# A hybrid decoder layer on one core: seven block products two tiles earlier in the first FFN, with their results kept in PSUM

## Chip, cores and metric

One Trainium2 chip, one of its cores. The metric is the device time of one launch in microseconds, as the median of several runs. The engines are named as in the profile: PE is TensorE (matmul), PEld its weight loads, DVE is VectorE, ACT is ScalarE, POOL is GpSimd, SP is SyncE, which issues the DMA transfers.

## The reference

One layer of a decoder trunk is computed for 1024 prompt rows and for 8 single sample rows with a cache. Width is 1024, the FFNs are 2816 wide.

```python
def swiglu(x, w_gate, w_up, w_down):
    return (jax.nn.silu(x @ w_gate) * (x @ w_up)) @ w_down

def decoder_layer(x, ...):
    h = x + 0.5 * rmsnorm(swiglu(rmsnorm(x, lp['n_ffn1_pre']), lp['ffn1_gate'], lp['ffn1_up'],
                                 lp['ffn1_down']), lp['n_ffn1_post'])
    proj = rmsnorm(h, lp['n_mix_pre']) @ lp['w_in']
    ...  # differential attention (512 wide) and RWKV-7 time mixing (512 wide)
    mix = jnp.concatenate([ya, yb], axis=-1) @ lp['w_out']
    h = h + rmsnorm(mix, lp['n_mix_post'])
    h = h + 0.5 * rmsnorm(swiglu(rmsnorm(h, lp['n_ffn2_pre']), lp['ffn2_gate'], lp['ffn2_up'],
                                 lp['ffn2_down']), lp['n_ffn2_post'])
```

Everything is float32. In the kernel a matrix is held as a high part (rounded to the fp32r type) and a low part (what is left), and a product is the sum of three fp32r matmuls: high by high, high by low, low by high.

## The kernel before

**Stages.** The rows are cut into two halves of 520 (with the 8 sample rows) and 512. The trunk runs four phases: 0 and 1 are the first FFN for the first and the second half, 2 and 3 the second FFN. Between and beside them run the projection, the attention, the time mixing and the output product, as streams of their own. `s_trunk` (L1034) runs the phases. A phase takes the 22 tiles of 128 FFN columns in turn: `gate` and `up` (L1061, L1081) make the two products of a tile for two chunks of rows (256 and 264 columns of a matmul, 8 blocks of the input dimension by 3 = 24 matmuls each), VectorE and ScalarE make silu(gate) × up of them, and split the result in a high and a low part. `down` (L1166) multiplies the activations of a group of tiles by their rows of the third weight matrix and adds the result to a sum in SBUF. The groups of tiles are in `GROUPS` (L102); while one group's gate and up run, the down products of the group before follow.

**Seven block products.** In phases 0 and 3, from tile `FAST[ph]` on (L35: 8 in phase 0, 4 in phase 3), two tiles at a time go through `seven` (L1098). It writes the product of a pair (weights 1024 × 256, inputs 1024 × 520) as blocks of two by two and makes it from seven products of blocks in place of eight, twice: for the gates and for the ups. Each of the seven takes 12 matmuls (4 input blocks by 3) of 260 columns. For this the weights' blocks are added by `sums` (L940) and the inputs' blocks by `s_combine` (L994). The latter makes four sums t1 to t4 of the input's blocks, in four steps, split in high and low parts: in the trace the tiles comb_acc and comb_sq are the sums, comb_dreg and comb_T hold their high and low parts (t1 and t2 in comb_dreg, t3 and t4 in the two tiles comb_T). `seven` waits for all of that.

After each of its products VectorE adds the bank to one of four slots `v` in SBUF (L1145 to L1152). When a block of the result is complete, `gates` (L1115) multiplies it by the row norms `rb` (phase 0), takes the tanh on ScalarE and multiplies; `ups` (L1123) multiplies the gates by it, ScalarE casts the high part into the ring of activations (trunk_xl in the trace) and VectorE or GpSimd subtracts it to get the low part. Six banks of PSUM rotate for the products (m0 to m3, aux0, aux1).

**The order.** Nothing is issued in the order of the source. Each operation goes through one helper (line L325 in every row of the profile) into a queue of its stream, and `Kern.run` (L484) plans all engines by a model of costs and due times: on each engine the operation that can start first goes first, and among those within a few hundredths of a microsecond the one with the earliest due time. `either` (L432) chooses VectorE or GpSimd for an elementwise operation by the same model. The due times come from a pass before; `PASSES` (L96) counts the planning passes (L2665), and the cheapest of all but the first is built. So a change in one place can move operations anywhere in the program.

Of the kernel before, what the change touches and what calls it, by code (L numbers as in the profile page):

```python
# [13 lines left out]
F32 = mybir.dt.float32  # L14
# [4 lines left out]
ALU = mybir.AluOpType  # L19
# [12 lines left out]
SAMPLE = slice(HS, HS + TD)  # L32
CHUNKS = [[(0, 256), (256, 264)], [(0, 256), (256, 256)], [(0, 256), (256, 256)], [(0, 264), (264, 256)]]
WIDE = (1, 2)
FAST = {0: 8, 3: 4}  # L35
HALF = 260
FOUR = 1
PIECE = 2048
# [54 lines left out]
MW = 1  # L93
MARG = 0
SLACK = 0.02
PASSES = 8  # L96
BIAS = {}
SHIFT = {}
MIX = 1
# [118 lines left out]
class Kern:  # L218
# [637 lines left out]
    def plan(ph):  # L856

        groups = [[0, 1, 2], [3, 4], [5, 6]] + [list(range(g, g + 3)) for g in range(7, NF, 3)]
        if ph in FAST:
            groups = GROUPS[ph, FAST[ph]] + [[g, g + 1] for g in range(FAST[ph], NF, 2)]  # L860
        down = lambda gi: [("down", gi, m0) for m0 in range(0, KT, Kern.down_tiles(groups[gi]))]
        seq = []
        for gi, grp in enumerate(groups):
            for q, f in enumerate(grp):
                if f < FAST.get(ph, NF):
                    seq += [("gate", f, None), ("up", f, None)]
# [10 lines left out]
    def s_weights(self):  # L877
# [3 lines left out]
        for ph in range(4):  # L881
# [4 lines left out]
            for n, (kind, f, m0) in enumerate(seq):  # L886
# [7 lines left out]
                if kind[-1] == "s":  # L894
                    yield from self.sums(ph, kind, f, m0, tag, last)
                    continue
                fast = kind == "down" and groups[f][-1] + 1 >= FAST.get(ph, NF + 1)
                if fast and not FOUR:
# [24 lines left out]
                kept = None  # L923
                if ph // 2 in LOWS and (kind == "down" or f < FAST[3 * (ph // 2)]):
                    kept = self.Ld[ph // 2][grp[0]:grp[-1] + 1, :, m0 * P:m0 * P + nm].rearrange("q p m -> p q m") if kind == "down" else \
# [108 lines left out]
    def s_trunk(self):  # L1034

        nc = self.nc
        V, A, G = nc.vector, nc.scalar, nc.gpsimd
        for ph in range(4):
            groups, _ = self.plan(ph)
            if ph in FAST:  # L1040
                self.spawn(self.s_combine(ph), "comb", 3)
# [13 lines left out]
            def weights(*key):  # L1055
                if key not in got:
                    yield ("wait", ("loaded", ph) + key)
                    got[key] = self.W.pop((ph,) + key)
                return got[key]
# [38 lines left out]
            def seven(f):  # L1098

                yield ("wait", ("combined", ph))  # L1100
                if ph == 0:
                    for c in range(2):
                        yield ("wait", ("rb", c))
                gt[:] = [self.T(self.pool, [P, 2 * W], j) for j in "gt"]
                b11, b21, b22, t1, t2, t3, t4 = self.blocks
                for i in range(2):
                    acts[f + i] = act[(f + i) % 4]

                def beside(fn, *a):
                    was = self.cur  # L1110
                    self.cur = self.asides["trunk"]
                    fn(*a)
                    self.cur = was

                def gates(i, j, src):  # L1115
                    g, t = gt[i][:, HALF * j:HALF * j + HALF], self.tmp("sq", 2, HALF)
                    if ph == 0:
                        V.tensor_tensor(g, src, self.rb[:, HALF * j:HALF * j + HALF], ALU.mult)
                        src = g
                    A.activation(t, src, AF.Tanh, scale=0.5)  # L1120
                    V.scalar_tensor_tensor(g, t, 1.0, src, ALU.add, ALU.mult)

                def ups(i, j, src):  # L1123
                    g = gt[i][:, HALF * j:HALF * j + HALF]
                    o = 1040 * ((f + i) % 4) + HALF * j
                    ah, al = (ring[:, o + w:o + w + HALF] for w in (0, 520))
                    V.tensor_tensor(g, g, src, ALU.mult)
                    A.copy(ah, g)
                    self.either("tensor_tensor", al, g, ah.bitcast(F32), ALU.subtract)

                for kind, use in (("gates", gates), ("ups", ups)):
                    v = [self.vs[(self.nv + i) % len(self.vs)] for i in range(4)]
                    self.nv += 4
                    late = []
                    for n, (j, i, x) in enumerate(((0, 0, b11), (0, 1, b21), (1, 0, t2), (1, 1, t3), (2, 0, t4), (2, 1, t1), (3, 0, b22))):
                        wh, wl = yield from weights(kind, f, j)
                        ps = self.ps(HALF)
                        for k in range(4):
                            self.mm3(ps, wh[:, i, k, :], wl[:, i, k, :], x[0][k], x[1][k], k == 0, k == 3)
                            if k == 1:  # L1140
                                yield "pe"
                        if i or j == 3:
                            self.signal(("used", ph, kind, f, j))
                        was, late = late, []
                        if n == 0:  # L1145
                            A.copy(v[0], ps)
                        elif n == 5:
                            V.tensor_tensor(v[2], v[2], ps, ALU.add)
                            V.tensor_tensor(v[0], v[0], ps, ALU.add)
                        else:  # L1150
                            o, a = ((1, 0), (0, 0), (2, 0), (3, 2), (0, 0), (0, 0))[n - 1]
                            V.tensor_tensor(v[o], v[a], ps, ALU.add)  # L1152
                        q = {1: (0, 0, 1), 4: (1, 0, 3), 5: (1, 1, 2), 6: (0, 1, 0)}.get(n)
                        if q:
                            late.append((use, q[0], q[1], v[q[2]]))
                        for fn, *a in was:
                            beside(fn, *a)
                        yield "pe"
                    for fn, *a in late:
                        beside(fn, *a)  # L1160
                if f + 2 == NF:
                    self.signal(("ups", ph))
                    if ph == 0:
                        self.spawn(self.s_resid(ph), "resid", 0)
# [1510 lines left out]
```

## Time and profile before

| what | value |
|---|---|
| median of 3 runs | 2241.66 us (2240.61 to 2243.62) |
| the profiled execution's own time | 2243.7 us |
| its span | 2241.9 us, 42167 instructions |
| granted TensorE clock, mean | 0.994 |
| DMA | 338.84 MB, 151 GB/s over the span |

The span is the stretch from the first to the last instruction of the profiled execution. All engines run side by side; an engine's busy time is the sum of its instructions' durations, and the time of the kernel is set by the engine that never waits, or by the chain of waits from one engine to the next. Where a row says "[2.59 <-DVE mix_T L325]", the engine had been idle for 2.59 us and went on when VectorE had written the tile mix_T.

### The profile page before, as it was taken

To read this page: it belongs to the slowest core of one execution; us is meant where nothing else is said; L and a number is where in the kernel's file an instruction comes from. 1 tells how busy PE (TensorE), PEld (TensorE's weight loads), DVE (VectorE), ACT (ScalarE), POOL (GpSimd) and SP (SyncE) were. 2 spreads that over 40 slices of the span, in tenths; PEclk is the share of its full clock that TensorE was granted. 3 is DMA by queue.
4 is the path that set the end of the run, shared out by engine and by line. 5 is a ranking of instruction groups with operands and counts; after the bars stand their busy time and mean duration, and the time that the engine had idled before them with its cause. 6 is when DMAs were issued, how large, how long until landed. Compare 5 with 4: busy or idle time off the path is not lost. (4 is left out here: it accounts for less than half of the span.)

```text
span 2241.9 us, 42167 instructions
## 1 busy us (share of the span) xinstructions
PE 2187.3 (98%) x15551; PEld 1960.6 (87%) x15551; DVE 1559.9 (70%) x3608; ACT 1085.1 (48%) x2233; POOL 1007.8 (45%) x834
## 2 busy tenths in 40 slices
PE   8999999999999989999999999999999999999998
PEld 8999998899887778898887777778888989999998
DVE  7868887656667787647775667776765366777776
ACT  6434444644553347344454445435655455444444
POOL 4545555533333673456453332335443355444443
PEclk9999999999999999999999999999999999999999
DMA  7322233445343674755564534476337838342343
GB/s 262 111 95 87 94 113 124 132 149 140 100 116 103 190 213 132 218 156 164 164 205 156 145 115 129 136 221 199 114 103 220 275 115 290 118 151 99 138 147 108
DMA packets 216088, 338.84 MB, mean 151 GB/s; under 512 B 50731, under 2 KB 130379, under 8 KB 215883
## 3 DMA queue, kind: packets, MB, share of 16 engines
q1 hardware_dynamic: 215594, 335.63, 47.9%
q8 instruction: 123, 2.02, 0.4%
q14 instruction: 83, 0.67, 0.1%
q10 hardware_dynamic: 288, 0.52, 0.1%
HBM read 281.06 MB, written 55.03 MB: 150 GB/s over the span
## 5 line engine op out<-in xcount | busy, mean ns | idle before, releaser
L325 POOL TENSOR_TENSOR wts_w<-wts_raw,wts_w 128x1024 fp32r<-128x1024 f32 (+2 forms) x160 | 301.2, 1886 | 356.8 <-ACT wts_w L325 301.1
L325 PE MATMUL trunk_m<-trunk_xl,wts_w 128*128 128x256 f32 (+2 forms) x2574 | 421.7, 316 | 0.4 <-DVE trunk_xl L325 0.4
L325 PE MATMUL trunk_m<-pre_X,wts_w 128*128 128x512 f32 (+3 forms) x2040 | 390.0, 344 | 9.6 <-ACT wts_w L325 6.0
L325 PEld LDWEIGHTS trunk_m<-trunk_xl,wts_w 128*128 128x128 f32 x2574 | 359.3, 188 | 29.4 <-issue 1.6
L325 PE MATMUL trunk_m<-pre_T,wts_w 128*128 128x512 f32 (+3 forms) x1800 | 364.6, 353 | 6.7 <-DVE trunk_xl L325 6.6
L325 PEld LDWEIGHTS trunk_m<-pre_X,wts_w 128*128 128x128 f32 x2040 | 312.8, 190 | 51.7 <-ACT wts_w L325 6.0
L325 ACT CAST wts_w<-wts_raw 128x512 fp32r<-128x512 f32 (+3 forms) x299 | 242.3, 826 | 211.1 <-PE trunk_m L325 123.0
L325 PEld LDWEIGHTS trunk_m<-pre_T,wts_w 128*128 128x128 f32 x1800 | 285.1, 191 | 47.3 <-issue 4.9
L325 PE MATMUL proj_m<-tail_xl,lin_w 128*128 128x256 f32 (+2 forms) x1920 | 320.9, 322 | 0.5 <-DVE init_E L325 0.5
L325 PEld LDWEIGHTS proj_m<-tail_xl,lin_w 128*128 128x128 f32 x1920 | 270.7, 188 | 35.0 <-issue 9.6
L325 DVE TENSOR_TENSOR trunk_xl<-trunk_xl,trunk_m 128x256 f32<-128x256 f32 (+2 forms) x362 | 172.5, 490 | 53.1 <-PE trunk_m L325 52.2
L325 POOL TENSOR_TENSOR lin_w<-lin_raw,lin_w 128x1024 fp32r<-128x1024 f32 x41 | 99.7, 2432 | 221.4 <-ACT lin_w L325 211.4
L325 POOL TENSOR_TENSOR trunk_xl<-trunk_t,trunk_xl 128x260 fp32r<-128x260 f32 (+3 forms) x87 | 93.7, 1078 | 132.9 <-ACT trunk_xl L325 128.9
L325 DVE TENSOR_TENSOR wts_w<-wts_raw,wts_w 128x1024 fp32r<-128x1024 f32 (+3 forms) x109 | 114.1, 1052 | 13.9 <-ACT wts_w L325 13.5
L325 POOL TENSOR_TENSOR wts_w<-wts_lraw,wts_w 128x512 fp32r<-128x512 f32 x57 | 78.5, 1380 | 60.1 <-ACT wts_w L325 57.4
L325 ACT CAST lin_w<-lin_raw 128x1024 fp32r<-128x1024 f32 x52 | 54.5, 1047 | 74.6 <-PE proj_m L325 54.0
L325 PE MATMUL trunk_m<-comb_T,wts_w 128*128 128x260 f32 x660 | 84.7, 283 | 0.0
L325 PEld LDWEIGHTS trunk_m<-comb_T,wts_w 128*128 128x128 f32 x660 | 81.7, 188 | 0.0
L325 ACT CAST wts_w<-wts_lraw 128x512 fp32r<-128x512 f32 x100 | 58.7, 619 | 38.5 <-POOL wts_lraw L325 12.5
L325 PE MATMUL trunk_aux<-trunk_xl,wts_w 128*128 128x256 f32 (+1 forms) x546 | 75.1, 282 | 0.0
L325 ACT CAST trunk_xl<-trunk_t 128x512 fp32r<-128x512 f32 (+3 forms) x94 | 45.4, 484 | 50.4 <-DVE trunk_t L325 49.7
L325 PEld LDWEIGHTS trunk_aux<-trunk_xl,wts_w 128*128 128x128 f32 x546 | 69.5, 189 | 0.0
(614 smaller groups left out, 4088.0 us busy)
## 6 DMA issues: line engine op xcount, KB each, us to landing
wts_raw<-in_ffn_gate_dram SPq DMA_DIRECT2D x87, 512.0 KB
wts_raw<-in_ffn_up_dram SPq DMA_DIRECT2D x56, 512.0 KB
lin_raw<-in_w_in_dram SPq DMA_DIRECT2D x52, 512.0 KB
wts_raw<-in_ffn_down_dram SPq DMA_DIRECT2D x52, 384.0 KB
wts_raw<-in_ffn_down_dram SPq DMA_DIRECT2D x31, 512.0 KB
wts_w<-Ld SPq DMA_DIRECT2D x22, 512.0 KB
wts_lraw<-in_ffn_down_dram SPq DMA_DIRECT2D x18, 512.0 KB
mix_T<-out_dram SPq DMA_DIRECT2D x36, 256.0 KB
```

What stands on the lines that cost most here:

```text
L325: o = Op(eng, lambda: fn(*a, **k), st)
```

## The change

Three parts. In phase 0 the seven block products begin with tile 6 in place of tile 8: the groups of tiles go from [0,1,2], [3,4], [5], [6,7] and seven pairs to [0,1,2], [3], [4,5] and eight pairs. The products' results stay in the bank of PSUM: two slots in SBUF in place of four for each kind, the sums that complete a block are written into the bank, and all that follows (norm, tanh, multiplication, cast, subtraction) reads it there; the subtraction is always VectorE's. And the planner makes nine passes in place of eight.

```diff
-FAST = {0: 8, 3: 4}
+FAST = {0: 6, 3: 4}
...
-PASSES = 8
+PASSES = 9
...
                     if ph == 0:
-                        V.tensor_tensor(g, src, self.rb[:, HALF * j:HALF * j + HALF], ALU.mult)
-                        src = g
+                        V.tensor_tensor(src, src, self.rb[:, HALF * j:HALF * j + HALF], ALU.mult)
                     A.activation(t, src, AF.Tanh, scale=0.5)
                     V.scalar_tensor_tensor(g, t, 1.0, src, ALU.add, ALU.mult)
...
-                    V.tensor_tensor(g, g, src, ALU.mult)
-                    A.copy(ah, g)
-                    self.either("tensor_tensor", al, g, ah.bitcast(F32), ALU.subtract)
+                    V.tensor_tensor(src, g, src, ALU.mult)
+                    A.copy(ah, src)
+                    V.tensor_tensor(al, src, ah.bitcast(F32), ALU.subtract)
 
                 for kind, use in (("gates", gates), ("ups", ups)):
-                    v = [self.vs[(self.nv + i) % len(self.vs)] for i in range(4)]
-                    self.nv += 4
+                    v = [self.vs[(self.nv + i) % len(self.vs)] for i in range(2)]
+                    self.nv += 2
...
                         elif n == 5:
-                            V.tensor_tensor(v[2], v[2], ps, ALU.add)
                             V.tensor_tensor(v[0], v[0], ps, ALU.add)
+                            V.tensor_tensor(ps, v[1], ps, ALU.add)
                         else:
-                            o, a = ((1, 0), (0, 0), (2, 0), (3, 2), (0, 0), (0, 0))[n - 1]
-                            V.tensor_tensor(v[o], v[a], ps, ALU.add)
-                        q = {1: (0, 0, 1), 4: (1, 0, 3), 5: (1, 1, 2), 6: (0, 1, 0)}.get(n)
+                            o, a = ((ps, 0), (v[0], 0), (v[1], 0), (ps, 1), None, (ps, 0))[n - 1]
+                            V.tensor_tensor(o, v[a], ps, ALU.add)
+                        q = {1: (0, 0), 4: (1, 0), 5: (1, 1), 6: (0, 1)}.get(n)
                         if q:
-                            late.append((use, q[0], q[1], v[q[2]]))
+                            late.append((use, *q, ps))
```

The program has 14147 matmul rows on TensorE in place of 14171 (192 of 256 and 264 columns fewer, 168 of 260 more), 3669 rows on VectorE (3600 before), 2110 on ScalarE (2100), 803 on GpSimd (836) and 1219 on SyncE as before. On GpSimd 62 subtractions into trunk_xl are gone, and some 30 low parts of weights have come in.

The first place is TensorE's queue at the first products of the first pair that read a combined input (comb_dreg and comb_T; in brackets the engines whose counters a row waits for). Before:

```order
L325 MATMUL trunk_aux_237_1870<-comb_dreg_530,wts_w_217_1693 128x260 [waits Activation_49]
L325 MATMUL trunk_aux_237_1870<-comb_dreg_530,wts_w_217_1693 128x260 x11
L325 MATMUL trunk_m_239_1887<-comb_T_92_531,wts_w_217_1693 128x260 [waits DVE_49,Activation_49]
L325 MATMUL trunk_m_239_1887<-comb_T_92_531,wts_w_217_1693 128x260
L325 MATMUL trunk_m_239_1887<-comb_T_92_531,wts_w_217_1693 128x260 [waits Pool_49]
L325 MATMUL trunk_m_239_1887<-comb_T_92_531,wts_w_217_1693 128x260 x9
```

And of the change:

```order
L325 MATMUL trunk_aux_197_1453<-comb_dreg_530,wts_w_177_1265 128x260 [waits Activation_49]
L325 MATMUL trunk_aux_197_1453<-comb_dreg_530,wts_w_177_1265 128x260 x5
L325 MATMUL trunk_aux_197_1453<-comb_dreg_530,wts_w_177_1265 128x260 [waits Activation_49]
L325 MATMUL trunk_aux_197_1453<-comb_dreg_530,wts_w_177_1265 128x260 [waits DVE_49]
L325 MATMUL trunk_aux_197_1453<-comb_dreg_530,wts_w_177_1265 128x260
L325 MATMUL trunk_aux_197_1453<-comb_dreg_530,wts_w_177_1265 128x260 [waits Activation_49]
L325 MATMUL trunk_aux_197_1453<-comb_dreg_530,wts_w_177_1265 128x260 [waits Pool_49]
L325 MATMUL trunk_aux_197_1453<-comb_dreg_530,wts_w_177_1265 128x260
```

The third product (comb_dreg is t2) waited only at its start; now it waits for VectorE, ScalarE and GpSimd in its midst too, the last time for GpSimd at its eleventh matmul.

The second place is GpSimd's queue at the end of `s_combine` (trunk_xl is a tile's activation, wts_w a weight split, init and pre the inputs). Before:

```order
L325 TENSOR_TENSOR trunk_xl_18_121<-trunk_t_1206,trunk_xl_18_121 128x264 [waits Activation_49]
L325 TENSOR_TENSOR comb_T_93_532<-comb_sq_544,comb_T_93_532 128x260 [waits Activation_49]
L325 TENSOR_TENSOR comb_acc_545<-comb_acc_545,pre_X_47_150 128x260 [waits DVE_49,Pool_49]
L325 TENSOR_TENSOR comb_sq_547<-pre_X_46_149 128x260 [waits Pool_49]
L325 TENSOR_TENSOR comb_sq_548<-pre_X_46_149,comb_acc_546 128x260 [waits DVE_49]
L325 TENSOR_TENSOR comb_dreg_530<-comb_acc_546,comb_dreg_530 128x260 [waits Activation_49]
L325 TENSOR_TENSOR wts_w_189_1461<-wts_raw_1384,wts_w_189_1461 128x1024 [waits DMAHW4_49,Activation_49]
```

And of the change:

```order
L325 TENSOR_TENSOR trunk_xl_18_121<-trunk_t_1304,trunk_xl_18_121 128x256 [waits Activation_49]
L325 TENSOR_TENSOR comb_T_93_532<-comb_sq_544,comb_T_93_532 128x260 [waits Activation_49]
L325 TENSOR_TENSOR comb_acc_545<-comb_acc_545,pre_X_47_150 128x260 [waits DVE_49,Pool_49]
L325 TENSOR_TENSOR comb_sq_547<-pre_X_46_149 128x260
L325 TENSOR_TENSOR wts_w_196_1442<-wts_lraw_1394,wts_w_196_1442 128x512 [waits DMAHW2_49,PE_49,Activation_49]
L325 TENSOR_TENSOR comb_sq_548<-pre_X_46_149,comb_acc_546 128x260 [waits DVE_49,Pool_49]
L325 TENSOR_TENSOR comb_dreg_530<-comb_acc_546,comb_dreg_530 128x260 [waits Activation_49]
```

A weight split, which waits for TensorE and for ScalarE's cast, has moved ahead of the last two steps of the combine.

The third place is VectorE's queue at the seam between the ups of a pair and the down products (trunk_aux1, m0, m1, m2 added to trunk_xl0 are down products; trunk_xl1 is the ring of activations; the number after a name's bank tells its use). Before:

```order
L325 TENSOR_TENSOR init_rb_10_113<-init_rb_10_113,trunk_aux0_320_2484 128x260
L325 TENSOR_TENSOR trunk_xl0_126_796<-trunk_xl0_126_796,trunk_aux1_324_2506 128x256
L325 TENSOR_TENSOR trunk_xl0_126_796<-trunk_xl0_126_796,trunk_m0_325_2514 128x264
L325 TENSOR_TENSOR wts_w3_319_2473<-wts_raw_315_2435,wts_w3_319_2473 128x512
L325 TENSOR_TENSOR trunk_xl0_126_796<-trunk_xl0_126_796,trunk_m1_326_2524 128x256
L325 TENSOR_TENSOR wts_cb_322_2494<-wts_raw_316_2436 128x512
L325 TENSOR_TENSOR trunk_xl0_126_796<-trunk_xl0_126_796,trunk_m2_327_2535 128x264
```

And of the change:

```order
L325 TENSOR_TENSOR trunk_aux0_224_1682<-init_rb_10_113,trunk_aux0_224_1682 128x260
L325 TENSOR_TENSOR trunk_m3_222_1660<-trunk_t_193_1414,trunk_m3_222_1660 128x260
L325 TENSOR_TENSOR trunk_xl0_126_786<-trunk_xl0_126_786,trunk_aux1_228_1704 128x256
L325 TENSOR_TENSOR trunk_xl1_18_121<-trunk_m3_222_1660,trunk_xl1_18_121 128x260
L325 TENSOR_TENSOR trunk_aux0_224_1682<-trunk_g_192_1413,trunk_aux0_224_1682 128x260
L325 TENSOR_TENSOR trunk_xl0_126_786<-trunk_xl0_126_786,trunk_m0_229_1715 128x264
L325 TENSOR_TENSOR trunk_xl0_126_786<-trunk_xl0_126_786,trunk_m1_230_1727 128x256
L325 TENSOR_TENSOR trunk_xl1_18_121<-trunk_aux0_224_1682,trunk_xl1_18_121 128x260
```

The last product of the ups, in the bank aux0, was added into SBUF in one step and the bank was free; now the sum, the multiplication and the subtraction all happen in the bank, and the sixth down product is the next to use it.

Elsewhere the streams are interleaved anew without a clear direction: in TensorE's queue, ahead of two of the attention's products (attn_m) that read mix_T, there stand 1 matmul of the trunk (2 before) and 2 (4 before).

## The prediction

> **What bounds the kernel now.** First the page's table of engines, then the busy time by stretch. In the second view each row is a stretch of the span; the columns are its length, then each engine's busy time with its instructions, the granted TensorE clock, the DMA share and GB/s.
>
> ```profile
> PE 2187.3 (98%) x15551; PEld 1960.6 (87%) x15551; DVE 1559.9 (70%) x3608; ACT 1085.1 (48%) x2233; POOL 1007.8 (45%) x834
> core 0: us, PE busy (x) PEld busy (x) DVE busy (x) ACT busy (x) POOL busy (x), PEclk, DMA share, GB/s
> 142.50:361.00 218.50, 218.50 (x1824) 218.50 (x1823) 184.38 (x394) 93.78 (x191) 121.55 (x100) 1.00 0.32 106
> 430.00:1164.00 734.00, 718.90 (x4964) 620.67 (x4963) 500.99 (x1235) 348.01 (x713) 334.84 (x261) 1.00 0.53 158
> 1164.00:1820.00 656.00, 642.38 (x4030) 529.58 (x4029) 420.60 (x1010) 326.82 (x695) 252.58 (x168) 1.00 0.54 162
> 1877.00:2220.00 343.00, 343.00 (x2851) 342.95 (x2849) 251.31 (x533) 154.73 (x319) 158.38 (x148) 1.00 0.41 144
> ```
>
> TensorE sets the time. In the two stretches of block products (the first and the last row) it has no idle time at all, so there only fewer or shorter matmuls shorten anything. Between them it idles 734.0 − 718.9 = 15.1 us and 656.0 − 642.4 = 13.6 us, 28.7 us in all; a gain from a better order can only come from there or from the edges.
>
> **Term 1, fewer matmuls.** Then the timeline of TensorE, where seven products replace tiles (start, duration, operation, count):
>
> ```profile
> 77.10 23.14 PE L325 MATMUL trunk_m<-pre_X,wts_w 128*128 128x256 f32 x192
> 100.07 11.64 PE L325 MATMUL trunk_m<-trunk_xl,wts_w 128*128 128x256 f32 x96
> 129.57 13.09 PE L325 MATMUL trunk_m<-pre_X,wts_w 128*128 128x256 f32 x108
> 142.50 1.60 PE L325 MATMUL trunk_aux<-pre_X,wts_w 128*128 128x260 f32 x12
> ...
> 172.71 1.60 PE L325 MATMUL trunk_m<-pre_X,wts_w 128*128 128x260 f32 x12
> ...
> 192.89 0.87 PE L325 MATMUL trunk_aux<-trunk_xl,wts_w 128*128 128x256 f32 x6
> 193.60 3.03 PE L325 MATMUL trunk_m<-trunk_xl,wts_w 128*128 128x264 f32 x24
> ```
>
> Two tiles done one by one are 2 × 2 × 2 × 24 = 192 matmuls: tiles 4 and 5 take 100.07 − 77.10 = 22.97 us, 0.1196 each. A pair by seven products is 2 × 7 × 12 = 168 matmuls: 192.89 − 172.71 = 20.18 us. The change swaps tiles 6 and 7 for one more pair; their down products stay in number. **−2.8 us**, and nothing else of the edit removes TensorE work. Their weight loads, four for a pair, come up to 35 us earlier too; the pairs at 142.5 to 361 ran beside a DMA share of 0.32 without a wait, so I cost them at zero, and one late load at the 6.0 us of term 4's second row.
>
> **Term 2, the combined inputs come late.** The first seven-pair starts 35 us earlier. In before its first product begins after 96 of the 108 matmuls at 129.57, at 141.1 (the second is the row at 142.50); now after tiles 4 and 5 and the down products of tile 3 (96 + 48 + 96 matmuls), at 77.10 + 240 × 0.1196 = 105.8. The block sums of the inputs were ready at 117.0:
>
> ```profile
> 116.23 0.77 DVE L325 TENSOR_TENSOR comb_T<-comb_sq,comb_T 128x260 fp32r<-128x260 f32 x2
> ...
> 94.67 0.75 POOL L325 TENSOR_TENSOR comb_acc<-comb_acc,pre_X 128x260 f32<-128x260 f32 x1 [1.01 <-DVE comb_acc L325]
> 94.88 0.83 DVE L325 TENSOR_TENSOR comb_sq<-pre_X 128x260 f32<-128x260 f32 x1
> 97.71 0.42 DVE L325 TENSOR_TENSOR comb_sq<-comb_sq,pre_X 128x260 f32<-128x260 f32 x1
> 98.05 0.42 DVE L325 TENSOR_TENSOR comb_sq<-pre_X,comb_acc 128x260 f32<-128x260 f32 x1
> ...
> 110.42 0.74 POOL L325 TENSOR_TENSOR comb_sq<-pre_X,comb_acc 128x260 f32<-128x260 f32 x1 [3.18 <-DVE comb_acc L325]
> 111.13 0.74 POOL L325 TENSOR_TENSOR comb_dreg<-comb_acc,comb_dreg 128x260 fp32r<-128x260 f32 x1
> ```
>
> So 24 us of slack are gone and the chain must be pulled forward by the planner. The third product is the first that reads a combined tile. It starts at 105.8 + 2 × 1.44 = 108.7 (12 × 20.18 ÷ 168 = 1.44 per product), and its eleventh matmul, which waits for GpSimd's last low part, is due 10 × 0.119 = 1.2 us later, at 109.9. In the new order GpSimd has a weight split ahead of that low part. That split waits for a ScalarE cast, which waits until TensorE has left the weight buffer at the end of the second product. What such a chain takes, from rows further on:
>
> ```profile
> 204.40 1.60 PE L325 MATMUL trunk_m<-pre_X,wts_w 128*128 128x260 f32 x12
> 204.66 0.62 ACT L325 CAST wts_w<-wts_raw 128x512 fp32r<-128x512 f32 x1 [0.95 <-PE trunk_m L325]
> 205.35 1.29 POOL L325 TENSOR_TENSOR wts_w<-wts_raw,wts_w 128x512 fp32r<-128x512 f32 x1 [2.86 <-ACT wts_w L325]
> 1820.91 2.37 POOL L325 TENSOR_TENSOR wts_w<-wts_raw,wts_w 128x1024 fp32r<-128x1024 f32 x1 [1.94 <-ACT wts_w L325]
> 1823.34 3.50 PE L325 MATMUL trunk_m<-pre_X,wts_w 128*128 128x512 f32 x14 [1.45 <-POOL wts_w L325]
> ```
>
> From the end of the products to the cast 204.66 − 204.40 = 0.26, cast to GpSimd 0.69, the split 1.29, then the two steps of the combine at 0.71 (111.13 − 110.42) and 0.74, then to TensorE 1823.34 − (1820.91 + 2.37) = 0.06: 3.75 us. From 108.7 that is 112.4 against 109.9: **+2.5 us**, the third product waiting.
>
> Bounds. Below: nothing, if the ScalarE cast of the weights were not behind the second product after all (as in before, where the combine ended 24 us ahead). Above: VectorE and GpSimd slow each other when both read two tiles of SBUF: the subtraction at 94.88 took 0.83 us beside GpSimd's at 94.67, and 0.42 alone (97.71). If they went strictly in turn after the last elementwise step of tile 5 at 106.2, VectorE's eight rows left there (7 × 0.34, the step from 97.71 to 98.05, and 0.6) and GpSimd's seven (6 × 0.72 and 1.29) would sum to 8.6 us: 114.8, a stall of 4.9. I take 2.5, since it is the chain that the order itself imposes.
>
> Nothing else is queued between these on TensorE: the products behind are its own, so a stall there is time lost in full. What does a stall do to the clock?
>
> ```profile
> 824.31 0.50 PE L325 MATMUL attn_m<-mix_X 128*128 128x512 f32 x1 [2.59 <-DVE mix_T L325]
> 824.00:828.00 4.00, 3.69 (x16) 3.04 (x17) 3.67 (x7) 3.48 (x10) 1.51 (x1) 1.00 0.70 231
> 1870.10 7.59 PE L325 MATMUL trunk_m<-pre_T,wts_w 128*128 128x264 f32 x48 [2.77 <-DVE trunk_xl L325]
> 1870.00:1874.00 4.00, 3.90 (x20) 3.93 (x21) 3.13 (x8) 2.64 (x3) 3.57 (x5) 0.60 1.01 385
> 380.31 11.66 PE L325 MATMUL trunk_m<-pre_T,wts_w 128*128 128x512 f32 x38 [3.85 <-DVE trunk_xl L325]
> 378.00:382.00 4.00, 1.69 (x4) 1.43 (x5) 3.96 (x8) 0.96 (x4) 1.60 (x2) 0.65 0.00 0
> 382.00:386.00 4.00, 4.00 (x11) 3.04 (x11) 3.96 (x9) 0.22 (x1) 3.82 (x6) 0.50 0.01 4
> ```
>
> After a gap of 2.59 us the granted clock stayed 1.00; after 2.77 it was 0.60 for 4 us, 1.6 us lost; after 3.85 it was 0.65 and 0.50, 1.4 + 2.0 = 3.4 us lost. A stall of 2.5 lies just under the smallest that cost anything, so I add nothing. The Trainium skill ("TensorE: Matmul & The Clock Gate", What's actually happening) puts the window at about 3.4 us, free-running, and advises no gaps longer than that; by it alone a 2.5 us stall is free. The row at 1870.10 differs: 2.77 us did cost. Going by that row the forecast would be 1.6 us more.
>
> **Term 3, results that stay in PSUM.** The elementwise steps read and write a bank in place of SBUF:
>
> ```profile
> L325 DVE TENSOR_TENSOR init_E<-init_E,trunk_m 128x260 f32<-128x260 f32 x24 | 10.1, 423 | 8.8 <-PE trunk_m L325 8.7
> L325 DVE TENSOR_TENSOR wts_dec<-wts_cb,wts_raw 128x512 f32<-128x512 f32 x16 | 11.1, 692 | 0.0
> 194.88 0.68 DVE L325 TENSOR_TENSOR wts_w<-wts_raw,wts_w 128x512 fp32r<-128x512 f32 x1
> L325 POOL TENSOR_TENSOR trunk_xl<-trunk_g,trunk_xl 128x260 fp32r<-128x260 f32 x30 | 25.2, 839 | 38.3 <-ACT trunk_xl L325 38.3
> L325 POOL TENSOR_TENSOR trunk_xl<-trunk_t,trunk_xl 128x260 fp32r<-128x260 f32 x32 | 24.7, 772 | 32.1 <-ACT trunk_xl L325 32.1
> ```
>
> Into PSUM an operation costs what it costs into SBUF (692 ns to a bank, 0.68 us at 194.88 to SBUF; 423 ns with a PSUM input, 0.42 without): zero per instruction. What moves is the last subtraction of each result: 62 of them (30 + 32) leave GpSimd for VectorE, some 4 per pair × 0.42 = 1.7 us in a pair of 20.18 + 11.6 = 31.8 us. VectorE is busy 184.4 of 218.5 us in this stage, 4.96 us free per pair, so it is hidden beneath TensorE; without that cover it would be 1.7 us × 17 pairs.
>
> What it can cost is a bank. Six banks rotate, and one is now held until its split is done. At the seam to the down products the bank of the seventh product is due again at the sixth down product, 5 × (193.60 − 192.89) = 3.6 us later. VectorE's first row after a product, and then its seven others until the split is done:
>
> ```profile
> 193.80 0.42 DVE L325 TENSOR_TENSOR trunk_xl<-trunk_xl,trunk_aux 128x256 f32<-128x256 f32 x1 [0.28 <-PE trunk_aux L325]
> ```
>
> 193.80 − 193.60 = 0.2 to start, 7 × 0.34, then 0.42: 3.0 us, slack 0.6. It just fits: zero. One weight split of 0.68 between them, as at 194.88, would overrun by some 0.1, with ScalarE's cast in between 0.2, at each of the 17 pairs of both FFNs: +3.4. Below zero it can't go, since TensorE does not wait there now.
>
> **Term 4, the plan made anew.** All streams are interleaved afresh (one pass more), with the same work outside the first FFN. What that moves in the middle is bounded by the waits of TensorE (total, times, longest):
>
> ```profile
> PE attn_m L325 <- DVE mix_T L325: 6.3, 4, 2.6
> PE trunk_m L325 <- ACT wts_w L325: 6.0, 1, 6.0
> ```
>
> Between −6.3 (the attention's waits all filled) and +6.0 (one long wait more). The new order puts fewer matmuls of the trunk ahead of two of these waits, and nothing in it says that others grow or shrink; I take 0, as the middle keeps its work.
>
> **Sum.** −2.8 + 2.5 + 0 + 0 = −0.3 us. The profiled execution took 2243.7 us (span 2241.9 and 1.8 around it), so 2243.4 by it; the median of the runs, 2241.66, is 2.0 lower, so **2241.4**.
>
> **Rivals.** A difference under 0.2%, 4.5 us here (2237.2 to 2246.1), is about what a measurement of this kernel can tell from no change.
> - A, the sum above, 2241.4: 0.43, same.
> - E, the combine is in time, only term 1 counts: 2238.9. For it: the planner knows when the inputs are due. Against it: the weight split ahead in GpSimd's queue. 0.10, same.
> - C, the bank seam overruns in each pair: −0.3 + 3.4, 2244.8. For it: slack of 0.6 only. Against it: 34 us of free VectorE time in the stage. 0.09, same.
> - B, the other side: GpSimd and VectorE go in turn at the end of the combine, the third product stalls 4.9 us and the clock falls as at 380.31, 3.4 us more. −2.8 + 4.9 + 3.4 = +5.5, 2247.2. Slower by 4.5 needs stall and clock of 7.3, so it decides from a stall of 3.9 us. For it: 0.83 beside GpSimd against 0.42. Against it: ScalarE's and GpSimd's waits leave gaps in which VectorE runs alone. 0.20, slower.
> - D, the new plan fills the attention's waits: −0.3 − 6.3, 2235.1. For it: 28.7 us idle in the middle. Against it: fewer FFN matmuls ahead there. 0.18, faster.
>
> **Range and chances.** Low is E's 2238.9 with D's 6.3 less, about 2233; high is B with most of C, about 2250; 1 to 2 in 10 are left outside. Faster 0.22 (D, and a part of E with a little of the middle), same 0.52, slower 0.26 (B, and A or C with a longer middle).
>
> **What would show it.** Right: 24 matmuls fewer, the first 260-column product near 106 us, one TensorE gap of about 2.5 us in the third product, put down to GpSimd's combined tile, the clock at 1.00 after it, and no gaps in the following pairs. Wrong: no gap there (E), a gap of 4 us with a clock near 0.5 behind it (B), a short gap before the sixth down product of each pair (C), TensorE's idle time between the FFNs far from 28.7 us (D, or its opposite).

## The result, and the profile after

The changed kernel took 2227.64 us (median of four, 2225.54 to 2232.84) against 2242.64 us before: a ratio of 0.9938, 95% interval 0.9923 to 0.9954. It is 15 us faster where 0.3 us was forecast, and outside the range of 2233 to 2250. In a second comparison the ratio was 0.9949 (0.9936 to 0.9963). The profiled execution is the slowest of the four, 2232.84 us, with a span of 2231.1; so the two traces account for 2241.9 − 2231.1 = 10.8 us of the 15. The other three had spans of 2223.8 to 2225.9 us and a granted clock of 0.995 to 0.996 in place of 0.994, and no trace of them exists.

The page of the changed kernel, table of engines:

```profile
PE 2185.9 (98%) x15527; PEld 1957.8 (88%) x15527; DVE 1553.5 (70%) x3677; ACT 1082.2 (49%) x2243; POOL 1001.3 (45%) x801
```

TensorE's busy time fell by 1.4 us and its idle time by 9.4 (from 2241.9 − 2187.3 = 54.6 to 45.2). The gain is waiting that went. Where, is read best by cutting both spans at the same three events: TensorE's first matmul of phase 1, of phase 2 and of phase 3. The first and the last of the four stretches hold all block products, so all that the change touches; the two in the middle (phase 1, the projections, the attention, the time mixing, phase 2) hold none of them. Busy time by stretch, before and after (columns as in the prediction):

```profile
0.00:380.31 380.31, 367.78 (x3025) 365.23 (x3025) 304.50 (x692) 178.61 (x369) 192.21 (x175) 1.00 0.39 128
380.31:1116.51 736.20, 721.10 (x4964) 622.41 (x4964) 498.51 (x1234) 351.27 (x715) 338.65 (x265) 0.99 0.50 151
1116.51:1870.10 753.59, 735.73 (x4568) 610.99 (x4569) 490.27 (x1117) 383.32 (x799) 305.86 (x229) 1.00 0.55 166
1870.10:2241.90 371.80, 362.69 (x2996) 361.93 (x2996) 266.58 (x568) 171.86 (x353) 171.09 (x165) 0.99 0.42 145
```

```profile
0.00:380.00 380.00, 368.59 (x3001) 365.64 (x3001) 304.85 (x733) 181.41 (x379) 188.13 (x163) 0.99 0.38 126
380.00:1107.20 727.20, 717.71 (x4965) 618.77 (x4964) 498.83 (x1239) 348.50 (x714) 347.34 (x267) 1.00 0.51 153
1107.20:1859.32 752.12, 737.66 (x4568) 612.91 (x4569) 477.33 (x1111) 382.91 (x796) 312.72 (x234) 0.99 0.54 165
1859.32:2231.10 371.78, 361.91 (x2999) 360.51 (x2997) 272.46 (x596) 169.38 (x357) 153.16 (x139) 0.99 0.43 148
```

The stretches with the changed operations: 380.31 to 380.00, and 371.80 to 371.78. The second stretch, with the same number of matmuls within one (a record or two can be missing), went from 736.2 to 727.2: **9.0 of the 10.8 us lie where the change has no operation at all.** Other traces of the same two orders bear this out. after_again (below), a second profile of the changed program, has 730.0 in this stretch, and after_comb6, whose matmuls run in the same order, 726.5; before_outb6, in the order of the kernel before up to 1734 us, has 734.4. So one order scatters by two to four microseconds here, and the two orders stay apart.

**The first stretch** is three things that cancel: the saving of 2.8 us, a stall, and a better seam. The combined inputs came late, as TensorE's timeline of the changed kernel shows:

```profile
108.91 1.24 PE L325 MATMUL trunk_aux<-comb_dreg,wts_w 128*128 128x260 f32 x9
113.01 0.38 PE L325 MATMUL trunk_aux<-comb_dreg,wts_w 128*128 128x260 f32 x1 [2.86 <-ACT comb_dreg L325]
114.64 0.80 PE L325 MATMUL trunk_aux<-comb_dreg,wts_w 128*128 128x260 f32 x2 [1.24 <-POOL comb_dreg L325]
115.24 5.25 PE L325 MATMUL trunk_m<-comb_T,wts_w 128*128 128x260 f32 x24
120.33 1.62 PE L325 MATMUL trunk_m<-comb_dreg,wts_w 128*128 128x260 f32 x12
```

And its granted clock there (first of the last three columns):

```profile
112.00:116.00 4.00, 1.74 (x7) 1.55 (x8) 3.96 (x8) 1.23 (x4) 2.16 (x3) 0.67 0.00 0
116.00:120.00 4.00, 4.00 (x20) 4.00 (x20) 3.79 (x8) 1.52 (x3) 1.41 (x2) 0.50 0.02 4
```

The stall is 2.86 + 1.24 = 4.1 us. The clock granted behind it, 0.67 and 0.50, is 4 × 0.33 + 4 × 0.50 = 3.3 us short of full, but for a part of that time TensorE was still waiting. What was lost in all is read from the starts: these 36 matmuls took 120.33 − 108.91 = 11.4 us where 36 × 0.12 = 4.3 are usual. That is 7.1 us, 4.1 of waiting and 3.0 of slow matmuls.

Against that, the seam from phase 0 to phase 1 got better. Before, TensorE waited 1.10 us for the norm's sum and 3.85 us for a bank. Its row for the first wait, and then VectorE's timeline before, which shows why it waited for the second:

```profile
374.78 0.70 PE L325 MATMUL tail_aux<-trunk_acc,init_onesD 128*128 128x256 f32 x2 [1.10 <-DVE trunk_acc L325]
375.96 0.43 DVE L325 TENSOR_TENSOR trunk_acc<-trunk_acc,trunk_sq 128x264 f32<-128x264 f32 x1 [0.55 <-ACT trunk_sq L325]
376.31 0.76 DVE L325 TENSOR_TENSOR trunk_xl<-trunk_xl,trunk_m 128x264 f32<-128x264 f32 x2
377.74 1.76 DVE L325 RECIPROCAL tail_aux<-trunk_acc 128x256 f32<-128x256 f32 x1 [0.67 <-ACT trunk_acc L325]
379.41 0.41 DVE L325 TENSOR_TENSOR trunk_acc<-trunk_acc,trunk_sq 128x264 f32<-128x264 f32 x1
379.75 0.42 DVE L325 TENSOR_TENSOR trunk_xl<-trunk_xl,trunk_m 128x264 f32<-128x264 f32 x1
```

The changed kernel at the same seam, VectorE's rows and then TensorE's:

```profile
378.66 0.76 DVE L325 TENSOR_TENSOR trunk_xl<-trunk_xl,trunk_m 128x264 f32<-128x264 f32 x2
380.82 1.75 DVE L325 RECIPROCAL tail_aux<-trunk_acc 128x256 f32<-128x256 f32 x1
376.54 2.58 PE L325 MATMUL trunk_m<-trunk_xl,wts_w 128*128 128x264 f32 x19 [0.63 <-DVE trunk_xl L325]
380.00 13.61 PE L325 MATMUL trunk_m<-pre_T,wts_w 128*128 128x512 f32 x58
```

In the kernel before, the reciprocal of the norm (1.76 us) and its wait for ScalarE stood on VectorE ahead of the addition that empties the bank for phase 1 (379.75). In the new order those additions come first, and the reciprocal at 380.82 follows. Gaps of 4.95 us shrank to 0.63. So 7.1 − 2.8 − 4.3 = 0.0 us, where −0.3 was measured. The slow clock behind the gaps (0.65 and 0.50 in the prediction's rows at 378 to 386) went with them: before, the first 38 matmuls of phase 1 took 11.66 us, and at the changed kernel's pace, 13.61 ÷ 58, they would take 8.9. That is 2.7 us, and it counts in the next stretch.

**The second stretch** holds that 2.7 us, and the waits of the mixing. TensorE's timeline before, at two of them:

```profile
740.45 1.48 PE L325 MATMUL job_aux<-mix_X,bset_TT 64*64 64x128 f32 x16 [2.01 <-DVE mix_X L325]
817.00 0.44 PE L325 MATMUL attn_m<-mix_X 128*128 128x384 f32 x1 [2.37 <-DVE mix_T L325]
```

The clock before, behind the first:

```profile
740.00:744.00 4.00, 3.55 (x25) 3.23 (x26) 3.16 (x7) 1.24 (x5) 3.19 (x2) 0.63 0.49 132
744.00:748.00 4.00, 4.00 (x21) 2.80 (x21) 1.81 (x6) 0.38 (x2) 1.84 (x3) 0.52 0.75 222
```

Of TensorE's waits over the whole span (total, times, longest), the largest row before, then the changed kernel's rows that answer to it and to the attention's 6.3 us:

```profile
PE trunk_m L325 <- DVE trunk_xl L325: 8.0, 5, 3.8
PE trunk_m L325 <- DVE trunk_xl L325: 3.2, 7, 0.7
PE attn_m L325 <- DVE mix_T L325: 1.2, 2, 0.9
```

The gap of 2.01 us, with up to 4 × 0.37 + 4 × 0.48 = 3.4 us of clock behind it, is gone, and the attention's waits fell from 6.3 to 1.2 us. The waits for trunk_xl, the two seams among them, fell from 8.0 to 3.2. For this stretch that makes at most 2.7 + 5.4 + 5.1 = 13.2 us; 9.0 came out. Other waits grew by 1.5 us (all of TensorE's idle time in the stretch fell from 15.1 to 9.5), and its busy time fell by 3.4 where the two clock losses allow up to 6.1. That last difference of 2.7 us has no explanation here.

### The profile page after: what moved, and what is told of

Same layout as the page of the kernel before. It is cut to its first block, busy times and chain, and to the rows that moved or that the text cites. A ratio compares the mean times of both kernels' runs of the same rounds, so it can differ in the third digit from the quotient of the medians.

```text
span 2231.1 us, 42116 instructions
## 1 busy us (share of the span) xinstructions
PE 2185.9 (98%) x15527; PEld 1957.8 (88%) x15527; DVE 1553.5 (70%) x3677; ACT 1082.2 (49%) x2243; POOL 1001.3 (45%) x801
## 5 line engine op out<-in xcount | busy, mean ns | idle before, releaser
L325 POOL TENSOR_TENSOR wts_w<-wts_raw,wts_w 128x512 fp32r<-128x512 f32 (+2 forms) x188 | 336.7, 1799 | 395.3 <-ACT wts_w L325 337.2
L325 PE MATMUL trunk_m<-pre_X,wts_w 128*128 128x512 f32 (+3 forms) x1872 | 371.2, 350 | 7.3 <-ACT wts_w L325 5.7
L325 ACT CAST wts_w<-wts_raw 128x1024 fp32r<-128x1024 f32 (+3 forms) x300 | 240.5, 818 | 237.2 <-PE trunk_m L325 126.2
L325 PEld LDWEIGHTS trunk_m<-pre_X,wts_w 128*128 128x128 f32 x1872 | 293.5, 191 | 49.5 <-ACT wts_w L325 5.7
L325 POOL TENSOR_TENSOR trunk_xl<-trunk_t,trunk_xl 128x512 fp32r<-128x512 f32 (+2 forms) x49 | 60.9, 1244 | 109.1 <-ACT trunk_xl L325 109.0
L325 DVE TENSOR_TENSOR wts_w<-wts_raw,wts_w 128x1024 fp32r<-128x1024 f32 (+3 forms) x82 | 86.4, 1059 | 18.6 <-ACT wts_w L325 17.3
L325 PE MATMUL trunk_m<-comb_T,wts_w 128*128 128x260 f32 x708 | 92.9, 287 | 0.0
L325 PEld LDWEIGHTS trunk_m<-comb_T,wts_w 128*128 128x128 f32 x708 | 89.9, 193 | 0.0
L325 PE MATMUL trunk_aux<-trunk_xl,wts_w 128*128 128x264 f32 (+1 forms) x576 | 79.4, 283 | 0.0
L325 ACT CAST wts_w<-wts_dec 128x512 fp32r<-128x512 f32 x34 | 20.0, 588 | 115.1 <-DVE wts_dec L325 88.3
```

What stands on the lines that cost most here:

```text
L325: o = Op(eng, lambda: fn(*a, **k), st)
```

## The experiments

Three theories. **P**: the gain lies in the plan, that is in the order (and the choice between VectorE and GpSimd) which the planner happened to make of operations that the change leaves alone. **Q**: results in PSUM make it. **C**, for the kernels with all operations as they were: it comes from the changed operations, whatever the order. All ratios are against runs of the kernel before on the same chip; the stretches are those of the profiled executions, cut as above.

| kernel | median us | ratio (95%) | stretch 1 | 2 | 3 | 4 |
|---|---|---|---|---|---|---|
| before (profile above) | 2242.64 | | 380.3 | 736.2 | 753.6 | 371.8 |
| changed (profile above) | 2227.64 | 0.9938 (0.9923 to 0.9954) | 380.0 | 727.2 | 752.1 | 371.8 |
| after_again | 2230.72 | 0.9949 (0.9936 to 0.9963) | 378.8 | 730.0 | 753.6 | 371.7 |
| seven6_only | 2249.79 | 1.0036 (1.0023 to 1.0050) | 381.0 | 737.0 | 759.3 | 371.9 |
| psum_only | 2240.82 | 0.9994 (0.9982 to 1.0006) | 376.5 | 742.0 | 752.1 | 370.2 |
| passes8 | 2235.05 | 0.9975 (0.9965 to 0.9986) | 379.0 | 732.4 | 749.1 | 372.1 |
| before_plan2 | 2241.76 | 0.9998 (0.9982 to 1.0014) | 380.4 | 730.6 | 755.1 | 371.4 |
| before_plan5 | 2241.10 | 0.9995 (0.9983 to 1.0006) | 380.7 | 735.1 | 753.8 | 371.8 |
| after_plan9 | 2235.56 | 0.9976 (0.9964 to 0.9988) | 379.1 | 732.6 | 756.3 | 371.9 |
| groups345 | 2241.29 | 0.9999 (0.9985 to 1.0014) | 379.2 | 736.2 | 750.3 | 374.6 |
| after_attn10 | 2242.26 | 1.0003 (0.9987 to 1.0018) | 379.5 | 740.9 | 749.6 | 371.3 |
| after_job11 | 2248.67 | 1.0029 (1.0012 to 1.0047) | 379.9 | 745.9 | 749.6 | 371.4 |
| after_comb6 | 2230.17 | 0.9943 (0.9920 to 0.9965) | 378.9 | 726.5 | 751.3 | 371.3 |
| before_outb6 | 2237.83 | 0.9985 (0.9971 to 1.0000) | 381.0 | 734.4 | 748.7 | 371.6 |

**The change taken apart.** seven6_only is the kernel before with the two numbers alone, psum_only the changed kernel with the products from tile 8 on:

```diff
 # seven6_only, against before
-FAST = {0: 8, 3: 4}
+FAST = {0: 6, 3: 4}
-PASSES = 8
+PASSES = 9
 # psum_only, against the changed kernel
-FAST = {0: 6, 3: 4}
+FAST = {0: 8, 3: 4}
 # passes8, against the changed kernel
-PASSES = 9
+PASSES = 8
```

> The kernel before with the block products from tile 6 on (and nine passes), results still in SBUF. Theory P (the gain is in the plan: VectorE empties the banks ahead of the norm's reciprocal at the two seams between phases, which takes away the gaps of 3.85 and 2.77 us and the slow clock behind them): its queue on VectorE has both seams in the good order, and the combined inputs are as late as in the changed kernel, so about 2228, within 4 us of the changed kernel. Theory Q (results in PSUM make the gain): no gain, matmuls -2.8 and the late combine +7.5 against before, about 2246.

> The changed kernel with the block products from tile 8 on as before, results in PSUM. Theory P: the seam from phase 0 to 1 is good but that from phase 2 to 3 has one bank still behind the reciprocal as before, no 24 matmuls saved and no late combine, about 2236 (5 to 7 us under before). Theory Q: about 2230, all of the gain.

> The changed kernel with eight planning passes in place of nine. Another plan is built, with both seams in the good order. Theory P: within 4 us of the changed kernel, 2224 to 2232. If the ninth pass alone were the gain: about 2240.

> The changed kernel once more, on the same chip as the others: 2224 to 2231, with the stall at the combined tile (4.1 us in the profile seen) and a clock under 1.00 behind it in its first 130 us.

Neither half gives anything: the first is slower by 9 us, the second no different, and both together are 10 us faster. Q falls as the cause of the whole gain, since psum_only has none in its median, and P's numbers for these two fall as well. What the results in PSUM are worth by themselves isn't shown: in psum_only's profile the two stretches with the changed operations are 5.4 us shorter than before (4.1 of it at the first seam, whose gaps are 0.82 there), and the two others 4.3 longer. The good order at the two seams, from which they were made, is there in seven6_only, whose late combine stalls TensorE for 2.45 + 0.98 us, less than in the changed kernel, and it is 9 us slower all the same; the loss against the changed kernel stands in stretches 2 and 3 (737.0 and 759.3 against 727.2 and 752.1), where these two kernels have the same operations. So the seams alone are not it. passes8 lost half of the gain by a change of order alone; its 2235.05 lies a little beyond the range that P gave. The ninth pass on the kernel before would build the same program as eight do, so that is not a theory of its own.

**The same operations from other plans.** The planner keeps several plans; these kernels build another one.

```diff
 # before_plan2, before_plan5 (against before), after_plan9 (against the changed kernel)
-    nc = build(min(plans[1:], key=lambda p: p[0])[2], False)
+    nc = build(plans[2][2], False)      # or plans[5], plans[9], with PASSES 3, 6, 10
```

> The kernel before, the same operations, built from another of its eight plans (the third in place of the fourth). Only the order differs, and in it the seam from phase 0 to 1 has the bank-emptying additions ahead. Theory P (the plan makes the gain): another time without any other operation; the seam alone gives 4.95 us of gaps and 3.4 us of clock less some 2.7 us that stay, -5; the stages behind scatter by 5 either way, so 2230 to 2240. Theory C (the gain comes from the changed operations): within 3 us of before, 2238 to 2244.

> The kernel before from its sixth plan: the same operations, and both seams as bad as in before. Theory P: the seams stay, the stages behind scatter, 2236 to 2246, with the gap of 3.8 us at phase 1's start. Theory C: within 3 us of before.

> The changed kernel from a tenth plan: the same operations in another order. Theory P: the first 380 us within 2 us of the changed kernel, the rest may scatter, 2228 to 2240. Theory C: within 3 us of the changed kernel, 2228 to 2234.

Three orders of the kernel before are alike to 0.05% (0.9998 and 0.9995 of it), which speaks for C, and before_plan2 missed P's range, while before_plan5 fits both; three orders of the changed kernel are not (0.9949, 0.9975, 0.9976), which speaks for P, and after_plan9 lies in P's range and above C's. before_plan2 has no gap of 3.85 us at the seam, but six gaps of 0.3 to 1.1 us spread over the last products of phase 0, 3.1 us in all; its profiled second stretch is 5.6 us shorter, and no gain is left in the median. At this point nothing was settled, and the next runs leave every operation and most of the order alone.

**One number in the last planning.** Each shifts the due times of one stream by a few microseconds in the final planning only.

```diff
 # one of these, against the changed kernel (the last against before)
-SHIFT = {}
+SHIFT = {'attn10': [(0, 99999, -2.0)]}
+SHIFT = {'job11': [(0, 99999, 2.0)]}
+SHIFT = {'comb0': [(0, 99999, -6.0)]}
+SHIFT = {'outb0': [(0, 99999, -6.0)]}
```

> The changed kernel with the due times of one attention stream 2 us earlier in the last planning: the same operations, the same order up to the middle of the mixing, another order behind it. Theory P (the gain lies in the order of stages that the change doesn't touch): part or all of the gain goes, 2234 to 2242, and the loss stands between 380 us and the second FFN as idle TensorE time or a lower clock. Theory C (the changed operations carry the gain): within 3 us of the changed kernel, 2227 to 2234.

> The changed kernel with the due times of one time-mixing stream 2 us later in the last planning: the same operations, another order from the mixing on. Theory P: 2234 to 2244, with the first 380 us unchanged. Theory C: 2227 to 2234.

> The changed kernel with the due times of the input combine 6 us earlier in the last planning, little else moved: the combined tiles come earlier. If the late combine costs its gaps of 2.9 and 1.2 us and the clock behind them: the gaps shrink to 2 to 3 us in all, the first 380 us are 1 to 4 us shorter, and the whole is 2225 to 2231 if the order behind holds. If the stall is bound to the engines' work: gaps of 4 us as before.

> The kernel before with the due times of the output product's stream 6 us earlier in the last planning: the same operations, and the order differs from the second half on, with the seam from phase 2 to 3 good. Theory P: that gap of 2.77 us and its 1.6 us of clock go, 2236 to 2240 unless the order before it costs as much. Theory C: within 3 us of before.

These decide. after_attn10 has every operation of the changed kernel, and TensorE's order is the same, row by row, for the first 788 us; in after_job11 for the first 614. Up to there no time is lost: the last matmul of the common order starts at 787.8 us against 788.3 in the changed kernel, and at 613.9 against 614.1. Behind it the order differs, and some ten elementwise operations are VectorE's instead of GpSimd's in after_attn10 (3686 rows on VectorE in its trace, 3677 in the changed kernel's), fewer in after_job11 (3680). The whole gain is gone in the one (1.0003), and the other is slower than before (1.0029). The first lies 0.3 us above P's range, the second 5, and both far above C's. Busy time of after_attn10 by stretch, and behind the "..." in two pieces of the second:

```profile
0.00:379.49 379.49, 367.81 (x3000) 364.82 (x3001) 304.80 (x734) 180.98 (x379) 187.73 (x162) 0.99 0.38 127
379.49:1120.38 740.89, 725.36 (x4966) 622.53 (x4964) 505.95 (x1248) 350.84 (x716) 332.12 (x257) 0.99 0.49 150
1120.38:1869.94 749.56, 737.97 (x4569) 612.98 (x4569) 476.15 (x1111) 382.73 (x796) 314.10 (x234) 0.99 0.54 166
1869.94:2241.20 371.26, 361.88 (x2999) 360.53 (x2997) 271.72 (x596) 169.27 (x357) 152.87 (x139) 0.99 0.43 148
...
1004.00:1008.00 4.00, 1.82 (x9) 1.61 (x10) 4.00 (x8) 2.32 (x4) 4.00 (x5) 0.81 0.64 199
1008.00:1012.00 4.00, 3.75 (x9) 2.46 (x8) 4.00 (x6) 1.43 (x3) 3.77 (x4) 0.50 0.45 118
```

Stretches 1 and 4 are within some half a microsecond of the changed kernel's, and stretch 3 is 2.6 us shorter. Stretch 2 is 740.9 against 727.2: 13.7 us, of which 15.5 − 9.5 = 6.0 is idle time (length less TensorE's busy time) and the rest, 7.7, longer busy time. A part of that is a lower clock: 3.75 us busy at 0.50 are 1.9 us in the last row, and at 820 to 828 (0.77 and 0.81) up to 1.7 more are lost, where the changed kernel shows neither. At 1004 TensorE is busy for 1.82 of 4 us while VectorE has no free moment for 8 us, and the clock halves behind that. So C falls as well: the changed operations don't make the gain by themselves, and P stands in its general form. It does not follow that any part of the change makes a good order likelier; the six orders of the changed operations run here lie between 0.994 and 1.003, and two of them are plans that the planner's own model rates below the one that was built, so that stays open.

before_outb6 points the same way from the other side: the kernel before, every operation as it was, with the gap of 2.77 us at the second seam down to 0.17, is 0.9985 (0.9971 to 1.0000), some 3 us. That is in P's range, but C's "within 3 us" is met as well and the interval ends at 1, so it decides nothing.

**The late combine by itself.** after_comb6 (above) pulls the combine forward; groups345 gives it time by other groups of tiles:

```diff
-(0, 6): [[0, 1, 2], [3], [4, 5]]
+(0, 6): [[0, 1, 2], [3, 4], [5]]
```

> The changed kernel with the groups of tiles [0,1,2], [3,4], [5] in place of [0,1,2], [3], [4,5]: the same matmuls, but 48 down products more, 5.7 us, ahead of the first block products, which gives the combined inputs time. If the late combine costs what the profile shows (4.1 us and a clock loss of 1.7 to 3.4): the gap at the third product shrinks to under 2 us and the first 380 us get 4 to 7 us shorter, near 374; the whole follows unless the plan behind it scatters. If the stall is bound to the engines' total work and not to the time of the third product: a gap of 4 us again, a little later.

TensorE's timeline of groups345, then of after_comb6:

```profile
116.18 0.50 PE L325 MATMUL trunk_aux<-comb_dreg,wts_w 128*128 128x260 f32 x2 [0.16 <-POOL comb_dreg L325]
118.58 1.95 PE L325 MATMUL trunk_m<-comb_T,wts_w 128*128 128x260 f32 x14 [0.70 <-DVE comb_T L325]
136.05 0.62 PE L325 MATMUL trunk_m<-trunk_xl,wts_w 128*128 128x256 f32 x3 [1.10 <-DVE trunk_xl L325]
137.72 0.98 PE L325 MATMUL trunk_aux<-trunk_xl,wts_w 128*128 128x264 f32 x6 [1.06 <-DVE trunk_xl L325]
```

```profile
110.18 2.25 PE L325 MATMUL trunk_m<-pre_X,wts_w 128*128 128x260 f32 x12 [1.92 <-DVE trunk_t L325]
112.22 2.61 PE L325 MATMUL trunk_aux<-pre_X,wts_w 128*128 128x260 f32 x12
114.67 1.60 PE L325 MATMUL trunk_aux<-comb_dreg,wts_w 128*128 128x260 f32 x12
```

In both the stall at the third product is gone or nearly so, and in both time is lost elsewhere. In groups345 the first down products wait 1.10 and 1.06 us for VectorE, and the clock falls behind them (0.85 and 0.73 over 136 to 144, up to 1.7 us). In after_comb6 the first block product waits 1.92 us, and the next two products are slow (2.25 and 2.61 us where 1.60 is usual). The first stretch is 0.8 us shorter than the changed kernel's in groups345, where 4 to 7 were expected. In after_comb6 it is 1.1 shorter, the low end of the 1 to 4 expected, but after_again, with nothing moved, has the same 378.8. The stall seems to follow VectorE's work in this stretch more than the time of the third product; that is a reading of these rows and not shown. No version clearly beats the changed kernel; after_comb6 equals it.

## Why the prediction was wrong, by its steps

**Term 4, the plan made anew, is the step that failed.** The forecast took 0, "as the middle keeps its work", between −6.3 and +6.0. The middle kept its work and yet went from 736.2 to 727.2 us. The working bounded it by two rows of the waits, one group that would fill or one long wait added, and left out three things. The largest row of that view, TensorE waiting 8.0 us for trunk_xl, wasn't in the bounds; it fell to 3.2. The 3.85 us gap at 380.31 was quoted for its clock alone, but it was itself a wait set by the order (a reciprocal ahead of an addition), with a price of 3.85 + 2.7 us. And the clock behind a gap, priced in term 2 (1.6 us behind 2.77), had no price here. What the runs showed in place of the 0 is a middle that the plan alone moves by more than the forecast's bounds: a small shift of due times moves the same operations by 0.54% and 0.80% against the changed kernel (1.0003 and 1.0029 against 0.9949), 12 and 18 us.

**Rival D** named a right place: the attention's waits fell by 5.1 of its 6.3 us, and TensorE's idle time in the two middle stretches from 33.0 to 24.0, its sign. The rest of the 9.0 us of the second stretch, the clock behind gaps above all, was not in its price. The argument against it, fewer matmuls of the trunk ahead of two of these products, pointed the wrong way.

**Term 1** held in number: the first stretch has 3025 − 3001 = 24 matmuls fewer. Its 2.8 us can't be seen by itself. In stretch 1 it is buried beneath the stall, and psum_only, which lacks the saving and the stall, has the shortest first stretch of all, 376.5 us. The 3.5 us between the two fit 7.1 − 2.8 = 4.3 to within a microsecond, which is too coarse to measure 2.8.

**Term 2** had the place and the sign right and the size too low. The third product began at 108.91 (108.7 forecast) and stalled 4.1 us in place of 2.5; and the clock behind it cost 3.0 us, where the forecast added nothing, because 2.5 was held to lie under the smallest gap that cost anything. The kernel before has a shorter one that did, 2.01 us at 740, which the working didn't look at. The chain was in part other than assumed. The wait of 1.24 us was for GpSimd's last low part, as forecast. The long wait, 2.86 us, was for ScalarE's cast, which waited for VectorE's sums. Those ran beside a combine step and the weight split of GpSimd, as the timeline of the changed kernel shows, VectorE's rows, then ScalarE's, then GpSimd's:

```profile
110.25 0.87 DVE L325 TENSOR_TENSOR comb_acc<-pre_X,comb_acc 128x260 f32<-128x260 f32 x1
111.14 1.37 DVE L325 TENSOR_TENSOR comb_acc<-comb_acc,pre_X 128x260 f32<-128x260 f32 x1
112.55 0.41 ACT L325 CAST comb_dreg<-comb_acc 128x260 fp32r<-128x260 f32 x1 [1.98 <-DVE comb_acc L325]
110.09 0.73 POOL L325 TENSOR_TENSOR comb_sq<-pre_X 128x260 f32<-128x260 f32 x1
110.79 1.45 POOL L325 TENSOR_TENSOR wts_w<-wts_lraw,wts_w 128x512 fp32r<-128x512 f32 x1
```

VectorE took 0.87 and 1.37 us for steps of 0.42. The first ends at 111.12, 0.30 behind GpSimd's step (110.82), the second at 112.51, 0.27 behind the split (112.24). The Trainium skill ("SBUF — State Buffer", Who interferes with whom) says that a GpSimd instruction that reads SBUF and a VectorE operation with two SBUF inputs contend for a shared port, where one waits until the other has finished. These rows agree. This is **rival B's** mechanism, with its stall above the 3.9 us at which it was to decide and 4.1 + 3.0 − 2.8 = +4.3 us at its place. It decided nothing, since the rest of the program outweighed it. Rival E, the combine in time, fell.

**Term 3** held within 2 us. The last stretch, with the nine pairs of phase 3, took 371.78 us in place of 371.80. Before, it held the 1.6 us of slow clock at 1870, which the changed kernel doesn't have; but before_outb6, with the old operations and a small first gap, took 371.6 too. **Rival C** fell: in the changed kernel's TensorE timeline the down products of two pairs in a row start 31.69 us apart (first two rows), as before (third row: 193.60 − 161.95 = 31.65):

```profile
134.03 3.03 PE L325 MATMUL trunk_m<-trunk_xl,wts_w 128*128 128x264 f32 x24
165.72 3.03 PE L325 MATMUL trunk_m<-trunk_xl,wts_w 128*128 128x264 f32 x24
161.95 3.03 PE L325 MATMUL trunk_m<-trunk_xl,wts_w 128*128 128x264 f32 x24
```

## What to carry to other kernels

Where a planner orders the whole program anew, any edit is also a draw of a new order, and its size has to be measured with the operations held still: here a shift of 2 us in one stream's due times was worth up to 18 us, and the 2.8 us that the edit saves could not be seen beside it. Before a gain is put down to an edit, cut both spans at the same events and see whether the time went in stretches that the edit touches. And a gap of TensorE has two prices, its length and the clock behind it; look at seams between phases for a long step (here a reciprocal) standing ahead of the short one that empties a bank.

## What the runs showed of the hardware

The clock does not go by the length of a single gap. Behind 2.59 us at 824 it stayed at 1.00; behind 2.01 us at 740 it fell short by 3.4 us; and in after_attn10 it fell to 0.50 at 1008 behind four short waits, the longest 1.44 us, with TensorE busy for nearly half of the 4 us ahead. The losses came in steps: 1.6 us at 1870, 3.3 to 3.4 at 112, 378 and 740, and 5.1 at 1455 to 1471 in the changed kernel (0.87, 0.50, 0.50 and 0.85 over 4 us each). These count the granted clock; TensorE loses less where it waits meanwhile, 3.0 of the 3.3 at 112.

By the Trainium skill ("TensorE: Matmul & The Clock Gate", What's actually happening) the gate looks at activity in windows of about 3.4 us that run free of the program. As an estimate from that figure, one, two and three such windows at half speed lose 1.7, 3.4 and 5.1 us. The losses agree with that, and so does the missing relation to one gap's length. The same page's rule of no idle gaps above some 3.4 us (HAM oscillation — how this bites in real kernels) is too generous for the row at 740.

Executions of one kernel spread over 7 to 22 us (2225.2 to 2232.0 in after_comb6, 2240.1 to 2262.3 in after_job11). The mean granted clock of each execution is on record, and in each of the twelve runs above time and clock go against each other: in seven6_only 2242.4 us at 0.995 and 2256.8 at 0.989, where 0.006 of 2250 us would be 13.5 of the 14.4 between them. So much of the spread goes with the clock; the two profiles of the changed kernel also differ in where it fell. Why it falls more in one execution than in the next stays open.
